# Attention: probabilities times values in plain f32, even and odd key blocks in two 64-column tiles, instead of high and low parts

## The chip, the cores and the metric

The kernel runs on one core of a Trainium2 chip. The metric is the device time of one execution in microseconds (us); lower is better. The engines are named as in the profile: PE multiplies matrices, DVE and ACT work element by element and can read PSUM, POOL works element by element on SBUF, SP starts the transfers. Every engine takes its instructions in its own order.

## The reference

Two layers over 2048 positions of width 1024, batch 1, all in float32. Layer 0 runs a recurrent branch and an attention branch side by side; layer 1 is a state-space layer. The change lies in the attention of layer 0: 8 heads of 64 value columns, causal, keys of 96 (64 and 32 rotated).

```python
def _mla_attention(q_nope, q_rope, k_nope, k_rope, v):
    scale = (MLA_NOPE + MLA_ROPE) ** -0.5
    for blk in range(seqlen // Q_BLOCK):
        ...
        s = (jnp.einsum('bqhd,bkhd->bhqk', q_nope[:, q0:kend], k_nope[:, :kend])
             + jnp.einsum('bqhr,bkr->bhqk', q_rope[:, q0:kend], k_rope[:, :kend]))
        s = jnp.where(mask, s.astype(jnp.float32) * scale, -jnp.inf)
        p = jax.nn.softmax(s, axis=-1).astype(v.dtype)
        outs.append(jnp.einsum('bhqk,bkhd->bqhd', p, v[:, :kend]))
```

The result of the attention is multiplied by a gate and then by an output matrix (`ab_w_out`), 1024 by 1024.

## The kernel before, in words

Most products run in a reduced f32 type (`F32R`) on operands that were split into a high and a low part: the high part is a cast to that type, the low part what the cast left out. `lo` (line 128) makes the low part by a subtraction, `mm3` (line 131) adds the three products high times high, high times low and low times high.

**Work before the attention.** `qkv_begin` and `phase_qkv` make the keys, the values and the queries from two compressed inputs. `vunit` (602) makes one block of 128 positions of all heads' values: three matmuls, then for even and for odd heads a cast on ACT to the high part and a subtraction on DVE for the low part, written to `W`, the large weight buffer of ten slots. There the values of one head and one key block are 128 columns: 64 high and 64 low, in an order that depends on the head's parity. Eight of the 16 value blocks are made in `qkv_begin`, eight in `phase_qkv` beside the first eight query units, whose results leave through four staging tiles `qf` and the queue of SP.

**The attention.** `phase_attn` goes through 32 groups (`GROUPS`): head pair `pr`, chunk `c` of 512 queries, head `e` of the pair. Chunk c sees 4c+4 key blocks of 128, of which the last four are cut by the diagonal. For each group it
- makes the scores of 128 queries against up to 512 keys (`bank`, three matmuls at 741 to 743 and a mask matmul at 745), takes their maxima on DVE (746) and the exponentials on ACT (762) into `prob`;
- transposes 128 by 128 blocks of `prob` on PE (`trans`, 786), up to four for one key block, since the product with the values needs the keys on the partitions;
- casts the transposed block on ACT (792) to a high part and subtracts on DVE (793, by way of line 129) for the low part, into six buffers, four in slots 8 and 9 of `W` and two in `ptx`;
- multiplies (`pv`, 815): the 128 columns of values, high and low together, stay in the array; the high part and then the low part of the probabilities pass through. The accumulator `acc` then has, in one half of its partitions, the values' high part times both parts, and in the other the values' low part times both;
- adds the two halves (821 on ACT, 827 on DVE), multiplies by the gate and by one over the row sum on POOL (824, 831), and stores (834).

**What sets the order.** The program is recorded in the order in which Python calls it. Scores of group n are interleaved with transposes of the group before (loop at 847): after each score bank so many transposes are taken that the ready ones are used up by the end of the group. A `tick` after each step lets deferred work come due: the cast `TL` units after its transpose, the subtraction one later, the exponentials `EL` later. A product follows its transpose `LAG` key blocks later. SP loads the keys of the next head pair (687), the queries two groups ahead (701), and the row sums' and the gate's tiles (811, 812) in between; POOL splits the queries (705 and 129).

**At its end** POOL splits six of the eight slots of output weights (`load_at` at 863) during the last nine groups, into the slots of `W` whose values are used up; the last two are split on ACT and DVE (`last_w`, 866), one of them before the last products are issued. `out0_mm` (916) then reads slot `kb` for block `kb`.

## Time and profile before

| | |
|---|---|
| time, median of 3 runs | 2680.13 us (2680.01 to 2687.45) |
| time of the profiled execution | 2678.24 us |
| its span | 2676.4 us |
| mean granted TensorE clock in it | 0.994 |
| attention in it, first score matmul to last product | 461 to 957 us |
| busy in the whole span: PE, DVE, ACT, POOL | 2610.1, 1749.6, 1531.1, 944.2 us |

The profile comes from one execution. A group of instructions has a line of the program, an engine, an operation, output and input by name, shape, count, and its busy time and mean. A matmul's duration in it holds the time until its result has left the array, so that matmuls which follow each other overlap; how often they follow shows in their start times. An f32 matmul and its loading of weights (PEld) are told apart; "x32" is the number of such records. An entry like `<-DVE W L129` names what ended a wait. In rows of time, the first number is the start in us from the span's start, the second how long the row lasts, to its last record's end.

### The profile page before, as it was taken

The page shows a single profiled execution, that of the slowest core. Times are in us where ns is not written, and L with a number is a line of the kernel's source. Part 1 is how long each engine was busy: PE and PEld are TensorE (multiplying, and loading weights), DVE is VectorE, ACT ScalarE, POOL GpSimd, SP SyncE. Part 2 cuts the span into 40 slices and gives each one's busy share as a digit, 9 for nine tenths or more (in the row PEclk, how much of TensorE's full clock was granted, in tenths as well). Part 3 has the DMA queues.
Part 4 walks back from the last instruction along what each step waited for, and adds up shares of the span by engine and source line. Part 5 has one row for each costly group of instructions (what it writes and reads, how often), then busy time and mean ns, then how long its engine had stood idle before and what let it go on. Part 6 is the DMA issues. An engine that isn't in the chain of part 4 may idle for free.

```text
span 2676.4 us, 40050 instructions
## 1 busy us (share of the span) xinstructions
PE 2610.1 (98%) x14504; PEld 2153.2 (80%) x14504; DVE 1749.6 (65%) x3245; ACT 1531.1 (57%) x3178; POOL 944.2 (35%) x880
## 2 busy tenths in 40 slices
PE   8999999999999999999999999999999999899998
PEld 6888987878787878788888888888888888778886
DVE  7767236878787867875667666666677567745532
ACT  5665335877777732234677766766677667642100
POOL 4446211132324544550334223432343222434421
PEclk9999999999999999999999999999999999999999
DMA  4223328241424456682334333433343333455421
GB/s 140 59 87 118 113 90 284 44 72 43 72 53 85 74 174 196 214 266 95 112 132 159 112 112 108 164 114 112 128 157 123 107 105 118 154 184 210 173 95 40
DMA packets 173111, 334.23 MB, mean 125 GB/s; under 512 B 31985, under 2 KB 90225, under 8 KB 169457
## 3 DMA queue, kind: packets, MB, share of 16 engines
q1 hardware_dynamic: 172912, 331.66, 39.8%
q8 instruction: 115, 1.88, 0.3%
q14 instruction: 84, 0.68, 0.1%
HBM read 245.82 MB, written 85.79 MB: 124 GB/s over the span
## 4 chain that ended last, share of the span: by engine, by line
PE 73%; DVE 10%; ACT 6%; DMA 5%; issue 3%; POOL 1%; SPq 0%; ACTq 0%; POOLq 0%; DVEq 0%
PE ps L1159 9%; PE ps L1161 9%; PE ps L1160 9%; PE ps L137 5%; PE ps L139 4%; PE ps L138 4%; PE ps L786 4%; PE ps L815 4%; PE ps L1409 3%; PE ps L1408 3%; PE ps L1407 3%; PE ps L1262 2%; PE ps L921 2%; PE ps L923 2%; PE ps L922 2%
## 5 line engine op out<-in xcount | busy, mean ns | idle before, releaser
L1159 PE MATMUL ps<-ring,W 128*128 128x512 f32 x768 | 304.6, 397 | 0.0
L1161 PE MATMUL ps<-ring,W 128*128 128x512 f32 x768 | 300.1, 391 | 0.0
L1160 PE MATMUL ps<-ring,W 128*128 128x512 f32 x768 | 299.2, 390 | 0.0
L746 DVE TENSOR_REDUCE mx<-ps 128x1 f32<-128x512 f32 (+3 forms) x320 | 193.5, 608 | 73.9 <-PE ps L743 48.7
L1281 POOL TENSOR_TENSOR y<-y,xs 128x512 f32<-128x512 f32 x60 | 78.8, 1313 | 427.6 <-DVE y L1280 427.6
L762 ACT ACTIVATE pr<-ps,mx 128x512 f32<-128x512 f32 (+3 forms) x320 | 198.5, 629 | 15.8 <-DVE mx L750 11.0
L1159 PE MATMUL ps<-W,ring 128*128 128x512 f32 x512 | 201.3, 393 | 0.0
L1161 PE MATMUL ps<-W,ring 128*128 128x512 f32 x512 | 200.3, 391 | 0.0
L1160 PE MATMUL ps<-W,ring 128*128 128x512 f32 x512 | 199.9, 390 | 0.0
L786 PE MATMUL ps<-cst,pr 128*128 128x128 f32 x1088 | 176.6, 277 | 8.1 <-ACT pr L762 5.9
L1212 ACT ACTIVATE e<-e,tab 128x128 f32<-128x128 f32 x512 | 156.4, 390 | 41.8 <-DMA e<-d_cs 41.8
L1161 PEld LDWEIGHTS ps<-ring,W 128*128 128x128 f32 x768 | 144.1, 188 | 31.2
L1159 PEld LDWEIGHTS ps<-ring,W 128*128 128x128 f32 x768 | 144.3, 188 | 29.7 <-ACT yo L1313 0.9
L1160 PEld LDWEIGHTS ps<-ring,W 128*128 128x128 f32 x768 | 144.4, 188 | 28.9
L129 DVE TENSOR_TENSOR W<-ps,W 128x512 fp32r<-128x512 f32 (+3 forms) x261 | 145.0, 561 | 30.8 <-ACT W L613 18.8
L786 PEld LDWEIGHTS ps<-cst,pr 128*128 128x128 f32 x1088 | 130.6, 142 | 42.0 <-ACT pr L762 11.0
L1127 ACT ACT_TABLE_LOAD x58 | 74.4, 1283 | 149.0 <-DVE xT L1125 79.2
L1392 ACT CAST ring<-ring 128x1024 fp32r<-128x1024 f32 x50 | 50.3, 1045 | 188.7 <-PE ps L1408 99.3
L129 POOL TENSOR_TENSOR ring<-ring 128x1024 fp32r<-128x1024 f32 (+1 forms) x41 | 84.5, 2062 | 189.0 <-ACT ring L1392 160.1
L792 ACT CAST W<-ps 128x512 fp32r<-128x512 f32 (+2 forms) x213 | 110.8, 526 | 67.0 <-PE ps L786 63.0
L129 POOL TENSOR_TENSOR W<-st,W 128x512 fp32r<-128x512 f32 (+2 forms) x70 | 111.4, 1598 | 105.0 <-ACT W L112 90.2
L1125 DVE SCALAR_TENSOR_TENSOR xT<-ps,vec,xT 128x509 f32<-128x509 f32 (+2 forms) x192 | 143.2, 746 | 5.0
(347 smaller groups left out, 7509.7 us busy)
## 6 DMA issues: line engine op xcount, KB each, us to landing
ring<-d_x1T SPq DMA_DIRECT2D x128, 512.0 KB, 7.4
e<-d_cs SPq DMA_DIRECT2D x64, 512.0 KB, 4.4
ring<-d_y SPq DMA_DIRECT2D x25, 1024.0 KB, 4.8
st<-in_w_dram SPq DMA_DIRECT2D x40, 512.0 KB, 5.7
d_x1T<-xt SPq DMA_DIRECT2D x32, 512.0 KB, 4.0
d_y<-yo SPq DMA_DIRECT2D x64, 256.0 KB, 4.9
st<-in_wo_dram SPq DMA_DIRECT2D x24, 512.0 KB, 3.8
xs<-in_xT_dram SPq DMA_DIRECT2D x23, 512.0 KB, 3.9
```

The lines of the kernel that those rows point to most:

```text
L129: eng.tensor_tensor(out=out, in0=src, in1=hi.bitcast(F32), op=ALU.subtract)
L137: self.nc.tensor.matmul(ps, ah, bh, start=(i == 0), stop=False)
L138: self.nc.tensor.matmul(ps, ah, bl, start=False, stop=False)
L746: v.tensor_reduce(out=m[:, kc:kc + 1], in_=ps[:, 0:nw], axis=AX.X, op=ALU.max, negate=True)
L762: nc.scalar.activation(out=prob[n][:, o:o + nw], in_=ps[:, 0:nw], func=AF.Exp, bias=nm, accum_out=acc)
L786: nc.tensor.transpose(ps[:, i * 128:i * 128 + 128], prob[n][:, o:o + 128], self.ident)
L792: self.later(TL, lambda: nc.scalar.copy(hl[:, 0, w], ps[:, w]))
L1125: v.scalar_tensor_tensor(out=dst, in0=src, scalar=w(k), in1=dst, op0=ALU.mult, op1=ALU.add)
L1159: nc.tensor.matmul(ps, ah, bh, start=(k == 0), stop=False)
L1160: nc.tensor.matmul(ps, ah, bl, start=False, stop=False)
L1161: nc.tensor.matmul(ps, al, bh, start=False, stop=(k == KB - 1))
L1212: nc.scalar.activation(out=e[:, hd], in_=e[:, hd], func=AF.Relu, scale=-1.0, bias=cs[:, hd:hd + 1])
```

## The change

The values stay whole f32 numbers: a value block is copied from PSUM by one instruction on ACT to a staging tile and brought to its place in `W` by a transfer on SP's queue (512 pieces of 512 bytes). They take four slots of `W` instead of eight. A transposed block of probabilities is copied once, as f32, by ACT for even and by DVE for odd key blocks, into a buffer `pts` of six places; the cast and the subtraction are gone. Products come for two key blocks at a time: the even block's matmul has the head's 64 value columns in one half of the array's columns and writes one half of the accumulator's partitions, the odd block's matmul has its 64 in the other half and writes the other. The sum of both halves is taken as before, except where chunk 0's odd blocks reach only columns from 128 on. `LAG` is 4 instead of 5, and a product is issued only behind an odd block. The slots of the output weights are renumbered (`WO`), so that seven are split on POOL from the tenth-last group on, and only one is left for the end.

```diff
 GROUPS = [(pr, c, e) for pr in range(4) for c in ((3, 0, 1, 2) if pr == 3 else (3, 2, 1, 0)) for e in range(2)]
 
 
-EL, TL, LAG, SLACK = 3, 1, 5, 4
+WO = (4, 5, 6, 7, 0, 1, 2, 3)
+
+
+EL, TL, LAG, SLACK = 3, 1, 4, 4
+
+NPT = 6
 
 GL, GT, RT = 3, 3, 5
 
...
 
+    def values(self):
+
+        return self.W[:, 0:4, :].bitcast(F32).rearrange("p a (k n) -> p a k n", n=128)
+
     def qkv_begin(self):
 
         nc, A, v = self.nc, self.A, self.nc.vector
-        vv = self.W[:, 0:8, :].rearrange("p (a b) (k n) -> p a b k n", b=2, n=128)
+        vv = self.values()
         cT = self.cT
         self.cnt = 0
+        self.vtile = lambda: self.a2.tile([P, 512], F32, tag="cn", name="cn", bufs=4)
 
         def vunit(tt):
             c, t = divmod(tt, 4)
             ps = self.psum()
             s = cT[c][:, :, 2, t * 128:t * 128 + 128]
             self.mm3(ps, [((s[:, 0], s[:, 1]), (self.wkv[:, 0, 512:1024], self.wkv[:, 1, 512:1024]))])
-            p4 = ps.rearrange("p (a b n) -> p a b n", b=2, n=64)
 
             def post():
-                for b in range(2):
-                    hi = vv[:, :, b, tt, 64 * b:64 * b + 64]
-                    lo = vv[:, :, b, tt, 64 - 64 * b:128 - 64 * b]
-                    nc.scalar.copy(hi, p4[:, :, b])
-                    self.lo(v, lo, p4[:, :, b], hi)
+                f = self.vtile()
+                nc.scalar.copy(f, ps)
+                nc.sync.dma_start(out=vv[:, :, tt], in_=f.rearrange("p (a n) -> p a n", n=128))
             self.later(1, post)
 
         def kunit(pr, c):
...
     def phase_qkv(self):
         nc, p = self.nc, self.a3
         cT, D = self.cT, self.D
+        self.vtile = lambda: p.tile([P, 512], F32, tag="qf", name="qf", bufs=4)
         T = {}
 
         def factors(c):
...
 
     def phase_attn(self):
         nc, A, p, v = self.nc, self.A, self.at, self.nc.vector
-        vv = self.W[:, 0:8, :].rearrange("p h (k n) -> p h k n", n=128)
+        vv = self.values()
+        pts = p.tile([P, NPT, 512], F32, name="pts")
         ring, D = self.ring, self.D
         N = len(GROUPS)
 
         im = self.im
-        ptx = p.tile([P, 2, 1024], F32R, name="ptx")
 
         g, li, y = (p.tile([P, 512], F32, name=k) for k in ("g", "li", "y"))
         half = lambda e: slice(64 * e, 64 * e + 64)
...
                 o = 512 * c * i + 64 * i * (i + 1) + kb * 128
                 nc.tensor.transpose(ps[:, i * 128:i * 128 + 128], prob[n][:, o:o + 128], self.ident)
             self.cnt += 1
-            k = self.cnt % 6
-            hl = self.W[:, 8 + k // 2, k % 2 * 1024:k % 2 * 1024 + 1024] if k < 4 else ptx[:, k - 4]
-            hl = hl.rearrange("p (s n) -> p s n", s=2)
+            pt = pts[:, self.cnt % NPT]
             w = slice(128 * i0, 512)
-            self.later(TL, lambda: nc.scalar.copy(hl[:, 0, w], ps[:, w]))
-            self.later(TL + 1, lambda: self.lo(v, hl[:, 1, w], ps[:, w], hl[:, 0, w]))
-            flow.append((n, kb, hl, w))
+            copy = v.tensor_copy if kb % 2 else nc.scalar.copy
+            self.later(TL, lambda: copy(pt[:, w], ps[:, w]))
+            flow.append((n, kb, pt, w))
             if kb == 4 * c + 3:
                 prob[n] = None
-            if len(flow) > LAG:
+            if len(flow) > LAG and kb % 2:
                 pv()
             self.tick()
 
         def pv():
 
-            n, kb, hl, w = flow.pop(0)
+            (n, kb, *_), (_, kb1, *_) = two = [flow.pop(0) for _ in range(2)]
             pr, c, e = GROUPS[n]
             nkb = 4 * c + 4
             if kb == 0:
                 accs[n] = self.psum()
-            if kb == max(3, nkb - 8):
+            if kb == max(2, nkb - 8):
 
                 end[e]()
                 nc.sync.dma_start(out=li[half(e)], in_=D["li"][n].partition_broadcast(64))
                 nc.sync.dma_start(out=g[half(e)], in_=D["sg"][pr, half(e), c * 512:c * 512 + 512])
             acc = accs[n]
-            for s in range(2):
-                nc.tensor.matmul(acc[:, w], vv[:, 2 * pr + e, kb], hl[:, s, w],
-                                 start=(kb == 0 and s == 0), stop=(kb == nkb - 1 and s == 1))
-            if kb == nkb - 1:
-                r, o = half(e), half(1 - e)
+            r, o = half(e), half(1 - e)
+            for (_, b, pt, w), rows in zip(two, (r, o)):
+                nc.tensor.matmul(acc[rows, w], vv[:, pr, b, half(e)], pt[:, w], start=b < 2, stop=b >= nkb - 2)
+            if kb1 == nkb - 1:
+
+                w = slice(0 if c else 128, 512)
 
                 def copy():
-                    nc.scalar.copy(y[r], acc[o])
+                    nc.scalar.copy(y[r, w], acc[o, w])
+
+                def add():
+                    v.tensor_tensor(out=y[r, w], in0=y[r, w], in1=acc[r, w], op=ALU.add)
+                    if c == 0:
+                        v.tensor_copy(y[r, 0:128], acc[r, 0:128])
+                    accs.pop(n)
 
                 def gate():
                     nc.gpsimd.tensor_tensor(out=g[r], in0=g[r], in1=li[r], op=ALU.mult)
-
-                def add():
-                    v.tensor_tensor(out=y[r], in0=y[r], in1=acc[r], op=ALU.add)
-                    accs.pop(n)
 
                 def fin():
                     nc.gpsimd.tensor_tensor(out=y[r], in0=y[r], in1=g[r], op=ALU.mult)
...
                     trans()
             if pr < 3:
                 self.load_k(pr + 1, c, e)
-            k = n - (N - 9)
-            if 0 <= k < 6:
-                self.load_at(0, k, A["wo0"][k], 7, (nc.gpsimd, nc.gpsimd))
-        k, old, ws = 0, True, []
-
-        def last_w(i):
-            nc.scalar.copy(self.W[:, 6 + i, 0:1024], ws[i])
-            self.lo(v, self.W[:, 6 + i, 1024:2048], ws[i], self.W[:, 6 + i, 0:1024])
+            k = n - (N - 10)
+            if 0 <= k < 7:
+                self.load_at(0, WO[k], A["wo0"][k], 7, (nc.gpsimd, nc.gpsimd))
+        k, ws = 0, []
 
         def read_w():
-            for i in range(2):
-                ws.append(self.stp.tile([P, 1024], F32, tag="st", name="st"))
-                nc.sync.dma_start(out=ws[i], in_=A["wo0"][6 + i])
+            ws.append(self.stp.tile([P, 1024], F32, tag="st", name="st"))
+            nc.sync.dma_start(out=ws[0], in_=A["wo0"][7])
         todo = [(0, read_w), (1, lambda: [self.out0_load(tt) for tt in range(4)]),
                 (6, lambda: self.out0_split(0)), (8, lambda: self.out0_split(1))]
         while ready or flow or any(d[1].__qualname__.endswith("expo") for d in self.defer):
             while todo and todo[0][0] <= k:
                 todo.pop(0)[1]()
-            if old and k > 3 and not any(x[0] < N - 1 for x in ready + flow):
-                old = False
-                self.later(2, lambda: last_w(0))
             k += 1
             if ready:
                 trans()
...
                 self.tick()
         for _, fn in todo:
             fn()
-        if old:
-            last_w(0)
-        last_w(1)
+        hi, lo = self.W[:, WO[7], 0:1024], self.W[:, WO[7], 1024:2048]
+        nc.scalar.copy(hi, ws[0])
+        self.lo(v, lo, ws[0], hi)
 
         ps = self.out0_ps = [self.psum(), self.psum()]
         for hf in range(2):
...
         r, n0 = 2 * (tt % 3), half * 512
         for kb in range(k0, k1):
             ah, al = (self.ring[:, r + s, kb * 128:kb * 128 + 128] for s in range(2))
-            bh, bl = self.W[:, kb, n0:n0 + 512], self.W[:, kb, 1024 + n0:1536 + n0]
+            bh, bl = self.W[:, WO[kb], n0:n0 + 512], self.W[:, WO[kb], 1024 + n0:1536 + n0]
             self.nc.tensor.matmul(ps, ah, bh, start=(kb == 0), stop=False)
             self.nc.tensor.matmul(ps, ah, bl, start=False, stop=False)
             self.nc.tensor.matmul(ps, al, bh, start=False, stop=(kb == KB - 1))
```

PE's order in the attention, before the change, where a group with several chunks of keys is under way (786 transposes, 815 products, 741 to 743 scores):

```order
L786 MATMUL ps<-cst,pr 128x128 x4
L815 MATMUL ps<-W 128x512 x2
L741 MATMUL ps<-ring 128x512
L742 MATMUL ps<-ring 128x512
L743 MATMUL ps<-ring 128x512
L786 MATMUL ps<-cst,pr 128x128 x4
L815 MATMUL ps<-W 128x512 x2
L741 MATMUL ps<-ring 128x512
```

And after it, in such a place (794 transposes, 822 products, 749 to 751 scores):

```order
L794 MATMUL ps<-cst,pr 128x128 x4
L822 MATMUL ps<-pts,W 64x512 x2
L749 MATMUL ps<-ring 128x512
L750 MATMUL ps<-ring 128x512
L751 MATMUL ps<-ring 128x512
L794 MATMUL ps<-cst,pr 128x128 x4
L749 MATMUL ps<-ring 128x512
L750 MATMUL ps<-ring 128x512
L751 MATMUL ps<-ring 128x512
L794 MATMUL ps<-cst,pr 128x128 x4
L822 MATMUL ps<-pts,W 64x512 x2
```

Two products stood behind every transposed key block; now two stand behind every second one, of different key blocks. The 160 pairs come in 158 places, of which 128 have transposes ahead and scores behind, 29 transposes on both sides, and the last one three pairs in a row.

SP's order in the stage that makes the queries, after the change (702 and 695 load keys, 673 stores queries, 621 brings values to their place):

```order
L702 DMA ring<-d_kr 64x1024
L695 DMA ring<-d_k 64x1024
L673 DMA d_q<-qf 128x512
L621 DMA W<-qf 128x4x128
L702 DMA ring<-d_kr 64x1024
L695 DMA ring<-d_k 64x1024
L673 DMA d_q<-qf 128x512
L621 DMA W<-qf 128x4x128
```

The transfer of values is new in each of the first eight steps; before, the three others stood there without it.

## The prediction

> **What bounds the kernel now.** I read first the page's span and chain of waits, then the busy time per engine over the attention (461 to 957 us, first to last use of the changed lines), then PE's order in time inside it.
>
> ```profile
> span 2676.4 us, 40050 instructions
> PE 73%; DVE 10%; ACT 6%; DMA 5%; issue 3%; POOL 1%; SPq 0%; ACTq 0%; POOLq 0%; DVEq 0%
> ```
>
> ```profile
> core 0: us, PE busy (x) PEld busy (x) DVE busy (x) ACT busy (x) POOL busy (x), PEclk, DMA share, GB/s
> 500.00:550.00 50.00, 49.87 (x311) 42.74 (x310) 42.25 (x95) 39.09 (x101) 10.24 (x9) 1.00 0.25 43
> 550.00:600.00 50.00, 45.63 (x266) 38.27 (x264) 38.05 (x91) 34.74 (x99) 18.38 (x17) 0.97 0.51 81
> ...
> 461.00:957.30 496.30, 473.22 (x2821) 398.70 (x2819) 403.76 (x900) 376.28 (x998) 162.30 (x142) 0.99 0.36 69
> ```
>
> The chain is PE's for 73% of the span. In the attention PE is busy 473.2 of 496.3 us, so no more than 23.1 us there is idle; where the key blocks are many (500 to 550) it is busy 49.9 of 50, and the idle time sits where they are few (550 to 600). DVE (403.8) and ACT (376.3) have room. So the attention is PE's, and what matters is what PE does with the products of probabilities and values.
>
> **The products themselves.** The busy time of a matmul holds its latency, so I price by start to start. PE's order in time, columns start, time, engine, line:
>
> ```profile
> 522.29 0.60 PE L786 MATMUL ps<-cst,pr 128*128 128x128 f32 x4
> 522.65 0.71 PE L815 MATMUL ps<-W 128*128 128x512 f32 x2
> 523.20 0.39 PE L741 MATMUL ps<-ring 128*128 128x512 f32 x1
> 523.43 0.40 PE L742 MATMUL ps<-ring 128*128 128x512 f32 x1
> ...
> 523.89 0.60 PE L786 MATMUL ps<-cst,pr 128*128 128x128 f32 x4
> 524.25 0.59 PE L815 MATMUL ps<-ptx,W 128*128 128x384 f32 x2
> 524.68 0.34 PE L741 MATMUL ps<-ring 128*128 128x384 f32 x1
> ...
> 525.27 0.60 PE L786 MATMUL ps<-cst,pr 128*128 128x128 f32 x4
> 525.63 0.48 PE L815 MATMUL ps<-ptx,W 128*128 128x256 f32 x2
> 525.95 0.39 PE L741 MATMUL ps<-ring 128*128 128x512 f32 x1
> ...
> 526.65 0.60 PE L786 MATMUL ps<-cst,pr 128*128 128x128 f32 x4
> 527.01 0.42 PE L815 MATMUL ps<-W 128*128 128x128 f32 x2
> 527.26 0.44 PE L741 MATMUL ps<-ring 128*128 128x512 f32 x1
> ```
>
> From the first of four transposes to the next score matmul is 0.91 us. Four transposes take 0.44 (0.60 less the last one's own 0.27 is three steps of 0.11), so one key block's two products cost 0.47 at 512 columns; by the same subtraction 0.35 at 384, 0.24 at 256, 0.17 at 128. A group of chunk c has 4c+4 key blocks, the last four of them narrowing; over 32 groups that is 320 blocks: 96 pairs (512, 512), 32 pairs (512, 384) and 32 pairs (256, 128), at 0.94, 0.82 and 0.41.
>
> After the change a pair is two f32 matmuls of 64 columns in two tiles. The kernel has this form already, at L1262 with 64 moving columns, and a plain f32 matmul over the whole array at L1223:
>
> ```profile
> 1490.88 0.27 PE L1222 MATMUL ps<-cst,B 128*128 128x128 f32 x1
> 1490.99 0.39 PE L1223 MATMUL ps<-C,B 128*128 128x128 f32 x2
> 1491.13 0.47 PE L1159 MATMUL ps<-W,ring 128*128 128x512 f32 x1
> ...
> 1501.91 0.39 PE L1161 MATMUL ps<-ring,W 128*128 128x512 f32 x1
> 1502.23 1.15 PE L1262 MATMUL ps<-xf,e 128*64 128x64 f32 x32
> 1503.31 0.50 PE L137 MATMUL ps<-hl,ch 128*128 128x512 f32 x1
> 1503.65 0.39 PE L138 MATMUL ps<-hl,ch 128*128 128x512 f32 x1
> ```
>
> One f32 matmul is two records (L1223: one call, x2; L1262: 16 calls, x32). At 128 columns the second record starts 0.11 after the first (0.39 less one record's own 0.27 to 0.28). At L1262, 32 records start within 1.15 - 0.23 = 0.92 us: were they one after another, that would be 0.030 each, less than the 0.055 that half of 0.11 makes for 64 columns; so they run two at a time, one in each tile, 15 steps of about 0.06. A record of 512 columns is not in the trace. Four times the 128-column record is 0.44, eight times the 64-column step 0.49, the line through both 0.40; I take 0.43, near the row closest in kind per column, so 0.86 for a pair with 512 and 0.43 (twice 0.215) for (256, 128). Streams: 96 x (0.86 - 0.94) + 32 x (0.86 - 0.82) + 32 x (0.43 - 0.41) = **-5.8 us** (bounds: about -13 at 0.40 and +11 at 0.49). The sum of products costs PE almost what it cost.
>
> **The switch between tilings.** This is the term that decides. In the L1262 rows, L1161 to L138 is 1.74 us. In it are two matmuls of 0.23 (their usual step, as from L741 at 523.20 to L742 at 523.43) and 16 steps, 0.98. What is left, **0.30 us**, is paid once per visit: 0.09 before the first tile matmul (0.32 after L1161 instead of 0.23), the rest behind the last one, where L137 starts late and its follower comes 0.34 instead of 0.23 later, since the next weights were not loaded ahead. A visit of 64-column matmuls in one tile alone shows less:
>
> ```profile
> 990.68 0.39 PE L923 MATMUL ps<-W,ring 128*128 128x512 f32 x1
> 990.90 1.12 PE L1012 MATMUL ps<-xt,wdt 128*64 128x128 f32 x16
> 991.86 0.45 PE L921 MATMUL ps<-W,ring 128*128 128x512 f32 x1
> 992.15 0.40 PE L922 MATMUL ps<-W,ring 128*128 128x512 f32 x1
> ```
>
> 1.47 us, less 0.46 and 16 steps of 0.06, leaves 0.05. The Trainium skill says in TensorEngine Tiling (Array Packing), Key Properties, that changing the tiling mode, and not just the tile, drains TensorE. The trace agrees at L1262, and does not at L1012, whose columns are as few; a rule that held for every 64-column matmul would give 0.30 at both.
>
> The changed form is L1262's: f32, both tiles. PE's order shows one pair between transposes and scores nearly everywhere: 160 pairs in 158 visits. 158 x 0.30 = **+47.4 us** (bounds: 158 x 0.05 = +8, and +55 if the first weights, which L1262 also pays, come on top at 0.05). I take 0.30: same type, same two tiles.
>
> **What DVE and ACT get back.** Each transposed block had a cast on ACT (L792) and a subtraction on DVE (L129); now one copy, on ACT for even blocks and on DVE for odd ones.
>
> ```profile
> 461.00:957.30 496.30, 192.10 (x323) 57.26 (x44) 0.99 0.36 69
> ...
> 461.00:957.30 496.30, 165.53 (x320) 0.99 0.36 69
> ```
>
> The first row is L129 (DVE, POOL), the second L792 (ACT). DVE loses 192 us and, if a copy costs it what a subtraction did, gains back half, 96; ACT loses half of 165.5. That leaves DVE about 308 and ACT about 293 us busy of 496. That is not on PE's chain in the dense stretches. It can only shorten the 23.1 us of PE's idle time. The largest pieces of it, of three like this one, are:
>
> ```profile
> 573.76 0.59 PE L815 MATMUL ps<-W 128*128 128x384 f32 x2
> 576.93 0.33 PE L741 MATMUL ps<-ring 128*128 128x128 f32 x1 [2.58 <-POOL ring L705]
> ```
>
> There the queries' load is issued late, because in SP's queue it stood behind the store of the row sums, and that behind DVE's subtractions, as SP's waits from 540 to 585 us have it:
>
> ```profile
> SPq L775 <- DVE W L129: 2.7, 1, 2.7
> ```
>
> With DVE lighter, and PE slower by some 2 us on the way there, I take **-8 us** of stalls (bounds 0 and -23). The added wait is that of the pair for the copy on DVE; behind it on PE stand the next scores. It is covered: four transposed blocks, over 2 us of PE's work, lie between a copy and its product (LAG 4), against about 0.7 for the copy.
>
> **Values and weights.** Sixteen value blocks get one ACT copy and one 256 KB transfer in place of two casts and two subtractions; eight of these transfers fall where the DMA engines are full.
>
> ```profile
> 410.00:440.00 30.00, 29.62 (x124) 22.52 (x124) 15.51 (x30) 16.08 (x36) 0.00 (x0) 1.00 1.03 328
> ```
>
> DMA share 1.03 at 328 GB/s, PE still busy 29.6 of 30. Eight transfers of 256 KB at that rate are 6.4 us; the queries' four staging buffers now serve both, so part of it may reach PE. I take **+2** (bounds -1 and +6.4). At the end of the attention one of the two late splits of output weights no longer stands in front of the last copies:
>
> ```profile
> 954.30 0.50 PE L815 MATMUL ps<-W 128*128 128x512 f32 x1 [1.37 <-DVE W L129]
> ```
>
> That wait goes: **-1.4**. The seventh split on POOL (162 of 496 us busy) costs nothing.
>
> **Sum.** -5.8 + 47.4 - 8 + 2 - 1.4 = +34.2 on the profiled execution's 2678.2 (2676.4 of span) is 2712.4; that execution lies 1.9 under the median 2680.1, so **2714 us**, 1.3% slower. Own range of this case, by the bounds not all at one end: 2692 to 2745.
>
> **Rivals.**
>
> *The switch is cheap*, as at L1012. For it: no drain there, with as narrow weights. Against: another type and a single tile. Then -5.8 + 8 - 8 + 2 - 1.4 = -5, about 2675, no measurable change.
>
> *Relief decides, and it is faster.* If the switch is cheap and the lighter DVE and ACT also take 20 of the 23.1 us of idle time: -5.8 + 8 - 20 - 1.4 = -19, 2661. Its place is the groups with one or two chunks of keys, 550 to 600 and its like; it decides from the point where stalls won exceed 158 times the visit. At 0.30 they can't: 23 is less than 47.
>
> *The two tiles don't overlap.* L1262's two tiles read the same moving block xf; the change gives each tile another one. If that forces them one after another, each pair costs the second product too: 96 x 0.86 + 32 x 0.65 + 32 x 0.22 = +110, about 2824. For it, only that the trace shows no two streams of different data; against it, that each record of L1262 fetches its moving operand for itself. The Trainium skill gives in TensorE: Matmul & The Clock Gate, Measured speedup vs the span model, 2.38 times for three column tiles at 512 columns; an estimate from that page makes a pair 0.86 x 3 / 2.38 = 1.08 and the time near 2745. No run here shows it.
>
> **Chances.** Forecast 0.66; cheap switch 0.14; faster by relief 0.08; no overlap 0.12. The first two lie in 2668 to 2745 nearly whole, 0.79 together with the edges of the others; that is my range. A measurement of this kernel tells a change from none at about 0.3%, 8 us. Faster by more than that: 0.08 and a third of the cheap switch, 0.13. Within it: most of the cheap switch and the low edge of the forecast, 0.10. Slower: 0.77.
>
> **What would show it.** In the changed profile: two records of each tile starting together, about 0.43 apart, at the new product line (else the no-overlap rival); transposes to tile matmul and tile matmul to score matmul each about 0.1 later than their streams end, with the follower 0.34 instead of 0.23 behind (else the cheap switch); DVE near 308 and ACT near 293 us in the attention; the attention longer by some 33 us and everything after 960 us unchanged. The prediction is wrong if the attention is not longer, or by more than 65 us.

## The result and the profile after

The changed kernel takes 2709.73 us (median of 4 runs, 2704.89 to 2713.47) against 2681.48 us for the kernel before beside it (4 runs): a ratio of 1.010 with a 95% interval of 1.0074 to 1.0127, so 1% slower. The prediction was 2714 us. The profiled execution took 2704.89 us. The span and the chain of waits on the page of after:

```profile
span 2702.8 us, 39360 instructions
...
PE 80%; DVE 7%; DMA 5%; ACT 5%; issue 2%; POOL 1%; SPq 1%; ACTq 0%; POOLq 0%; DVEq 0%
```

Busy time by engine, the same three stretches as before (the last is the whole attention, which now begins at 470.1 us and ends at 983.3):

```profile
core 0: us, PE busy (x) PEld busy (x) DVE busy (x) ACT busy (x) POOL busy (x), PEclk, DMA share, GB/s
500.00:550.00 50.00, 50.00 (x279) 31.13 (x279) 29.64 (x67) 28.49 (x76) 12.01 (x11) 1.00 0.19 42
550.00:600.00 50.00, 49.76 (x292) 31.34 (x289) 29.06 (x75) 27.59 (x75) 13.69 (x13) 1.00 0.44 72
470.10:983.30 513.20, 502.78 (x2818) 323.82 (x2816) 321.71 (x747) 310.04 (x836) 164.18 (x145) 1.00 0.34 66
```

DVE and ACT fell by 82 and 66 us, as they should. PE is now almost without a gap even between 550 and 600 us (49.76 of 50), and the attention is 17.6 us longer all the same. Around one pair of products (columns start, time, engine, line):

```profile
521.79 0.60 PE L794 MATMUL ps<-cst,pr 128*128 128x128 f32 x4
522.32 1.08 PE L822 MATMUL ps<-pts,W 128*64 128x512 f32 x4
523.33 0.50 PE L749 MATMUL ps<-ring 128*128 128x512 f32 x1
523.67 0.40 PE L750 MATMUL ps<-ring 128*128 128x512 f32 x1
523.91 0.39 PE L751 MATMUL ps<-ring 128*128 128x512 f32 x1
```

Transposes to products: 0.53, of which 0.44 is the four transposes' own, so 0.09 late. The products stand for 1.01 until the score matmul; two records of 0.43 are 0.86, so 0.15 more. The follower comes 0.34 later instead of 0.23, 0.11 more. Together **0.35 us per visit**. The instruction records behind the row with x4 start in pairs, one in each tile, 6 to 7 ns apart (where the two blocks differ in width, the two records that start together have the two widths), and the second pair follows the first by 0.48: two tiles with different moving blocks do run side by side.

To see the rest I split PE's time in the attention in two. Every step from one matmul's start to the next is set against the usual length of such a step (the tenth percentile of steps with the same neighbours). The usual lengths add up to "work", what goes beyond them to "waits". Unlike PE's idle time, this also counts waits that are hidden in a matmul's latency and matmuls that run on a slower clock. The split depends a little on what counts as the same neighbours: where their widths must agree too, the groups are smaller and the waits come out at 46.5 and 18.6 us instead of 52.9 and 21.1. Differences of a few us between waits say nothing here.

| us | before | after | difference |
|---|---|---|---|
| attention begins | 461.6 | 470.1 | +8.5 |
| attention, work of PE | 442.7 | 492.1 | +49.4 |
| attention, waits of PE | 52.9 | 21.1 | -31.8 |
| behind the attention | 1719.2 | 1719.5 | +0.3 |
| span | 2676.4 | 2702.8 | +26.4 |

The work is 158 visits x 0.35 = +55.3, less 5.9 for the streams. The 8.5 us ahead of the attention arise where the value blocks are moved (the row of before for this stretch, 29.62 of 30 us busy, is in the prediction):

```profile
410.00:420.00 10.00, 8.76 (x36) 6.46 (x36) 1.21 (x2) 5.61 (x10) 0.00 (x0) 1.00 1.02 371
420.00:430.00 10.00, 6.18 (x16) 4.48 (x17) 1.38 (x2) 2.36 (x4) 0.00 (x0) 0.66 1.07 274
430.00:440.00 10.00, 7.05 (x29) 4.81 (x28) 2.07 (x3) 2.95 (x5) 0.00 (x0) 1.00 1.06 274
```

PE in the order of time there:

```profile
418.43 0.40 PE L144 MATMUL ps<-wkv,cT 128*128 128x512 f32 x1
423.82 0.79 PE L142 MATMUL ps<-cT,W 128*128 128x512 f32 x1 [4.99 <-ACT qf L672]
424.41 0.63 PE L143 MATMUL ps<-cT,W 128*128 128x512 f32 x1
```

The DMA engines are full (share 1.02 to 1.07). DVE waits 11.2 us for the store that empties a staging tile `qf`, ACT waits for DVE (7.4 us) and PE for ACT. Behind the wait the matmuls follow each other by 0.43 instead of 0.23: the granted clock is 0.66 in this slice. One trace each does not fix the 8.5 us to better than a few: in the traces of this case whose kernels have the same stages ahead of it, the attention begins at 461.6 to 465.3 us in the form of before (four traces) and at 469.3 to 476.6 in the form of after (eight).

Medians of the kernel before on the chips used below lie between 2681 and 2691 us. So I compare times by their ratio to the runs of before beside them, and, between traces, work and waits rather than tenths of a length.

### The profile page after: what moved, and what is told of

Its sections match the earlier page's. It is cut to its first block, busy times and chain, and to the rows that moved or that the text cites. A ratio compares the mean times of both kernels' runs of the same rounds, so it can differ in the third digit from the quotient of the medians.

```text
span 2702.8 us, 39360 instructions
## 1 busy us (share of the span) xinstructions
PE 2644.7 (98%) x14504; PEld 2082.8 (77%) x14504; DVE 1652.3 (61%) x3060; ACT 1464.1 (54%) x3001; POOL 944.4 (35%) x883
## 3 DMA queue, kind: packets, MB, share of 16 engines
q8 instruction: 114, 1.87, 0.3%
## 4 chain that ended last, share of the span: by engine, by line
PE 80%; DVE 7%; DMA 5%; ACT 5%; issue 2%; POOL 1%; SPq 1%; ACTq 0%; POOLq 0%; DVEq 0%
PE ps L1160 10%; PE ps L1162 10%; PE ps L1161 10%; PE ps L142 5%; PE ps L144 5%; PE ps L143 5%; PE ps L822 4%; PE ps L794 4%; PE ps L1409 4%; PE ps L1408 4%; PE ps L1410 4%; PE ps L749 2%; PE ps L1263 2%; PE ps L922 2%; PE ps L923 2%; PE ps L924 2%
## 5 line engine op out<-in xcount | busy, mean ns | idle before, releaser
L1160 PE MATMUL ps<-ring,W 128*128 128x512 f32 x768 | 304.7, 397 | 0.0
L1160 PE MATMUL ps<-W,ring 128*128 128x512 f32 x512 | 201.3, 393 | 0.0
L794 PE MATMUL ps<-cst,pr 128*128 128x128 f32 x1088 | 167.6, 275 | 4.7 <-ACT pr L770 4.7
L1160 PEld LDWEIGHTS ps<-ring,W 128*128 128x128 f32 x768 | 144.3, 188 | 29.6 <-ACT yo L1314 0.9
L799 ACT COPY pts<-ps 128x512 f32<-128x512 f32 (+1 forms) x160 | 86.9, 543 | 135.5 <-PE ps L794 134.3
L822 PE MATMUL ps<-pts,W 128*64 128x512 f32 (+3 forms) x640 | 158.1, 553 | 0.0
```

The source lines that it names most:

```text
L794: nc.tensor.transpose(ps[:, i * 128:i * 128 + 128], prob[n][:, o:o + 128], self.ident)
L822: nc.tensor.matmul(acc[rows, w], vv[:, pr, b, half(e)], pt[:, w], start=b < 2, stop=b >= nkb - 2)
L1160: nc.tensor.matmul(ps, ah, bh, start=(k == 0), stop=False)
```

## The experiments

### What a visit costs

**Half as many visits.** Four key blocks per visit instead of two, with room for eight transposed blocks; the gate's and the row sums' tiles move into `W`.

```diff
-NPT = 6
+NPT = 8
...
-        g, li, y = (p.tile([P, 512], F32, name=k) for k in ("g", "li", "y"))
+        y = p.tile([P, 512], F32, name="y")
+        g, li = (self.W[:, 8, 512 * k:512 * k + 512].bitcast(F32) for k in range(2))
...
-            if len(flow) > LAG and kb % 2:
+            if len(flow) > LAG and kb % 4 == 3:
+                pv()
                 pv()
...
-                    nc.gpsimd.tensor_tensor(out=g[r], in0=g[r], in1=li[r], op=ALU.mult)
+                    nc.gpsimd.tensor_tensor(out=y[r], in0=y[r], in1=li[r], op=ALU.mult)
```

> The changed kernel with products issued for four key blocks at a time (two pairs in a row) instead of two; buffers for transposed blocks 8 instead of 6, and to make room the gate and row-sum tiles lie in an unused slot of the weight buffer (the result is multiplied by the one and then by the other). The visits of PE to the 64-column tiles fall from 158 to 79; the products stay the same. Theory, the price is per visit (0.35 us each in the trace of the changed kernel: 0.09 before, 0.06 for the first weights, 0.09 behind, 0.11 for the follower): 79 x 0.35 = 28 us less, about 2677 against 2705. Rival, the price lies in the 64-column f32 products themselves: no change, 2705. Rival, longer visits hold up the scores and so DVE and ACT: part of the 28 us comes back as stalls, 2685 to 2700.

Measured: ratio 1.0079 (1.0053 to 1.0104). There are 79 visits, and PE's work fell from 492.1 to 463.8: 28.3 us, or 0.358 for each visit gone, as the expectation's theory has it. But the waits rose from 21.1 to 59.6 and the attention took 523.4, as its last rival has it and further. The gating had been changed too, so I repeated it with the gating left as it was.

**The same, with only the row sums' tile moved.**

```diff
-NPT = 6
+NPT = 7
...
-        g, li, y = (p.tile([P, 512], F32, name=k) for k in ("g", "li", "y"))
+        g, y = (p.tile([P, 512], F32, name=k) for k in ("g", "y"))
+        li = self.W[:, 8, 0:512].bitcast(F32)
...
-            if len(flow) > LAG and kb % 2:
+            if len(flow) > LAG and kb % 4 == 3:
+                pv()
                 pv()
```

> As visit2, four key blocks a visit, but with seven buffers for transposed blocks and only the row-sum tile moved to the unused weight slot, so that POOL multiplies the gate by one over the row sum ahead of the result, as in the changed kernel. In visit2 PE's work from start to start fell by 28.3 us in the attention as the theory had it, but its waits rose from 21 to 60 us, 26 us of them scores that waited for POOL's split of the queries. Theory, those waits came from the moved multiplication on POOL: they go here, the waits are near 21 us, the attention is near 485 us (513 less 28) and the time about 1% under the changed kernel's, level with the kernel before. Rival, waits grow because PE is faster and nothing hides them: PE's work 464 us, waits 40 us or more, attention above 500 us.

Measured: ratio 1.0086 (1.0068 to 1.0104). Work 464.2, waits 49.3, attention 513.5: to 0.3 us as long as after. This is the rival: with the gating left in place the waits are only 10 us lower. One visit of four blocks in PE's order:

```profile
521.45 0.60 PE L795 MATMUL ps<-cst,pr 128*128 128x128 f32 x4
521.98 1.94 PE L824 MATMUL ps<-pts,W 128*64 128x512 f32 x8
523.85 0.33 PE L750 MATMUL ps<-ring 128*128 128x128 f32 x1
```

It is again 0.53 to the products, and 1.87 for twice 0.86: the visit's cost is paid once, whatever its length. So the 0.35 us are a price per visit, and 28 us of them can be taken away; but in this kernel they come back as waits.

**Both products in one tile.** The odd block's product goes to the even one's columns, so the two run one behind the other; an even head uses one tile throughout, an odd head the other. The accumulator's halves are then not added (not in the lines below).

```diff
-            for (_, b, pt, w), rows in zip(two, (r, o)):
-                nc.tensor.matmul(acc[rows, w], vv[:, pr, b, half(e)], pt[:, w], start=b < 2, stop=b >= nkb - 2)
+            for _, b, pt, w in two:
+                nc.tensor.matmul(acc[r, w], vv[:, pr, b, half(e)], pt[:, w], start=b == 0, stop=b == nkb - 1)
```

> The changed kernel with both products of a pair in the same 64-column tile, one after the other, so that a group uses one tile alone, the first half of the columns for even heads and the second for odd ones; the accumulator's halves needn't be added. What it tells apart: the gaps of 0.09 us before and behind a visit. Theory A, they come from 64-column f32 products as such: they stay, for both halves. Theory B, they come from changing between two tile positions: they are gone for even heads at least, as at the reduced-f32 product of 64 columns in layer 0's last stage (0.05 in all). In both, the second product of each pair is no longer covered: 110 us more, attention about 620 us, time about 2815; if the tiles had not overlapped in the changed kernel, no more than now.

Measured, in a single run: 2815.01 us beside a median of 2687.6 before. Work 601.9, 109.8 more than after, which is what the prediction's rival without overlap put it at.

```profile
493.77 0.60 PE L794 MATMUL ps<-cst,pr 128*128 128x128 f32 x4
494.30 1.93 PE L822 MATMUL ps<-pts,W 128*64 128x512 f32 x4
496.16 0.50 PE L749 MATMUL ps<-ring 128*128 128x512 f32 x1
496.50 0.40 PE L750 MATMUL ps<-ring 128*128 128x512 f32 x1
```

0.53 ahead, 1.86 for the products, 0.34 for the follower. Ahead of the products every one of the 158 visits shows a step of 0.20 from the last transpose instead of 0.11, whether its tile is the first or the second half of the columns. So the price does not come from using two tiles, nor from changing between them.

The type alone could be a rival, since the products are f32 and the scores reduced. The kernel before settles it at L1223, f32 over the whole array with a reduced matmul behind it (the transpose ahead of it, at 1490.88, is in the prediction):

```profile
1490.99 0.39 PE L1223 MATMUL ps<-C,B 128*128 128x128 f32 x2
1491.13 0.47 PE L1159 MATMUL ps<-W,ring 128*128 128x512 f32 x1
1491.44 0.39 PE L1160 MATMUL ps<-W,ring 128*128 128x512 f32 x1
```

From 1490.88 to 1491.44 is 0.56, and the usual steps make 0.56 too: 0.11 for the transpose, twice 0.11 for the f32 records, 0.23 for L1159. L1160 comes late there as well (0.31 instead of 0.23), but L1159 had started as much too early, so nothing is paid. The 0.35 of a visit therefore holds only as a sum; its piece "follower 0.11 late" is in part the change of type, which starts the matmul ahead of it early. What is paid for is going from 128-column to 64-column matmuls and back, in f32. Why L1012, 64 columns in the reduced type, shows only 0.05 stays open.

### What the waits were

**Before without the subtractions.** The low part of the probabilities is left out: DVE makes none, and the second product uses the high part again. PE does the same number of matmuls.

```diff
-            self.later(TL + 1, lambda: self.lo(v, hl[:, 1, w], ps[:, w], hl[:, 0, w]))
...
-                nc.tensor.matmul(acc[:, w], vv[:, 2 * pr + e, kb], hl[:, s, w],
+                nc.tensor.matmul(acc[:, w], vv[:, 2 * pr + e, kb], hl[:, 0, w],
```

> The kernel before without its 320 subtractions on DVE in the attention: the second product of each key block reads the high part again, so that PE's and ACT's work stays and the probabilities' low part is left out. Theory, the 32 us of stalls that the change won back in the attention were mostly waits behind these subtractions, not behind the queue of SP at the change of head pairs: 18 to 28 us less than before, 2650 to 2660. Rival, DVE had room enough (404 of 496 us busy) and the stalls went because a slower PE hides them: within 5 us of 2678. Rival, half of it is ACT's casts: about 12 us less.

**After with a subtraction.** Each transposed block gets a subtraction on DVE again, whose result nobody reads.

```diff
             self.later(TL, lambda: copy(pt[:, w], ps[:, w]))
+            self.later(TL + 1, lambda: self.lo(v, self.W[:, 8, w], ps[:, w], pt[:, w]))
```

> The changed kernel with one more subtraction on DVE for each transposed block, as the kernel before had it; its result is not read. DVE's copies of odd blocks stay, so DVE has about 90 us more than before the change had. Theory, waits behind DVE decide the stalls: the attention gets 20 to 35 us longer, 2725 to 2740. Rival, a slower PE hides them: less than 8 us more, below 2713.

Measured: ratios 0.9937 (0.9922 to 0.9951) and 1.0167 (1.0148 to 1.0186). The attention of the first, then of the second:

```profile
463.70:946.00 482.30, 464.67 (x2817) 397.58 (x2816) 245.85 (x580) 373.36 (x998) 161.05 (x142) 0.99 0.39 71
```

```profile
476.60:1014.60 538.00, 512.97 (x2817) 327.21 (x2816) 477.92 (x1066) 309.37 (x836) 164.08 (x145) 0.99 0.35 64
```

Without the subtractions DVE is busy 245.9 instead of 403.5 us, and the waits fall from 52.9 to 39.2; the attention is 13.3 us shorter, below the 18 to 28 that were expected. With one added to after, DVE is busy 477.9 and the waits rise from 21.1 to 44.8; the work stays (493.1). So DVE's load is worth 13.7 us of waits measured from before and 23.7 measured from after (a load that is 18% above before's there). The change won 31.8; some 8 of them or more are something else. ACT's lighter load and PE's slower pace, which both changed too, were not tried apart.

### The values' way

**Values written by ACT straight into place**, without a staging tile and a transfer. They are rounded to the reduced type by it, so their low parts are left out.

```diff
-                f = self.vtile()
-                nc.scalar.copy(f, ps)
-                nc.sync.dma_start(out=vv[:, :, tt], in_=f.rearrange("p (a n) -> p a n", n=128))
+                nc.scalar.copy(self.W[:, 0:4, tt * 128:tt * 128 + 128], ps.rearrange("p (a n) -> p a n", n=128))
```

> The changed kernel without the sixteen transfers of values: ACT writes each value block straight to its place, rounded to the reduced f32 type, since that buffer takes no other from ACT. The values' low parts are left out by this; the count and size of PE's work stays. Theory, the 8.5 us by which the attention starts later than before come from these transfers in a stage whose DMA engines are full: the attention starts at about 462 instead of 470 us, and the time falls by 8 to 9 us to about 2696. Rival, they come from the staging tiles or from ACT's longer copies, or from the order of the queue of SP alone: less than 3 us.

Measured: ratio 1.006 (1.0038 to 1.0081). The attention begins at 456.3, 13.8 us earlier than after (8 to 9 were expected) and 5.3 earlier than before.

```profile
410.00:420.00 10.00, 10.00 (x44) 8.07 (x44) 2.50 (x4) 4.35 (x8) 0.00 (x0) 1.00 1.03 312
420.00:430.00 10.00, 10.00 (x45) 8.05 (x44) 2.20 (x4) 3.58 (x7) 0.00 (x0) 1.00 1.04 294
430.00:440.00 10.00, 8.60 (x37) 6.31 (x36) 4.13 (x6) 3.87 (x7) 0.00 (x0) 1.00 0.79 244
```

PE works almost without a gap. So the sixteen transfers, with the staging tiles that they hold, cost 13.8 us, and the lighter ACT and DVE give back some 5 of them; both by one trace each, and so to within a few us.

**The transfers spread out.** The shorter visits above, and the second half of the value blocks beside every fourth query unit instead of each of the first eight.

```diff
-            if n < 16 - 4 * VB:
-                self.vunit(4 * VB + n)
+            if n % 4 == 3:
+                self.vunit(4 * VB + n // 4)
                 self.tick()
```

> visit2b, with the eight value blocks of the query stage spread over its 32 steps (one in every four) instead of the first eight, so that their transfers do not all fall where the DMA engines are full and the staging tiles wait. Without any value transfers the attention started 13.8 us earlier. Theory, the transfers hold PE because they come in the full stretch: the attention starts 4 to 10 us earlier than the changed kernel's 470, and the time is 4 to 10 us under visit2b's, below the kernel before. Rival, the stage is limited by the sum of its transfers: no change against visit2b.

Measured: ratio 1.0078 (1.006 to 1.0096), against 1.0086 without the spreading; the attention begins at 471.5, no earlier. From 410 to 440 us PE is busy 21.27 of 30 and the DMA share is 1.04: as the rival has it, the stage goes by the sum of its transfers, and not by where they stand. That their sum is what holds it is argued from the full DMA engines; no run lessens the sum alone.

### Where the shorter visits' gain went

In the kernel with 79 visits and only one tile moved, the waits sit at the ends of the head pairs, where groups have few keys: 10.4 us of 49.3 fall between 575 and 600, 10.2 between 700 and 750, some 11 between 825 and 875. There:

```profile
584.45 0.38 PE L795 MATMUL ps<-cst,pr 128*128 128x128 f32 x2
590.33 0.47 PE L750 MATMUL ps<-ring 128*128 128x128 f32 x1 [5.50 <-POOL ring L713]
```

PE waits for POOL's split of the next queries, and POOL for the queries. I took SP's order for the cause: at 580 us SP stood 7.2 us at the load of the row sums, which waits for their store, with a queries' load behind it.

**The row sums one block earlier**, in the kernel before:

```diff
-            if kb == max(3, nkb - 8):
+            if kb == max(2, nkb - 8):
```

> The kernel before, with one number changed: for chunk 0 the row sums and the gate are fetched, and the work on the group two before is finished, one key block earlier (at block 2 instead of 3), where the changed kernel does it too. Theory, the three waits of 1.5 to 2.6 us at the change of head pairs and what follows them, some 10 us of the 32 us of waits that the change won back, come from that place: the scores' wait for POOL's split of the queries goes, the attention is 8 to 12 us shorter than before's 496. Rival, they come from ACT's or DVE's load or from PE's pace: less than 3 us.

Measured, in a single run: 2691.95 us beside a median of 2687.6; waits 61.4. The expected 8 to 12 us do not show.

**The queries' path taken out of the queues.** ACT and DVE split the queries instead of POOL; POOL's queue takes the loads of row sums and gate and the store of the output from SP's. It was done to three kernels: the one with 79 visits, after, and before.

```diff
-        nc.gpsimd.tensor_scalar(out=t[:, 0:512], in0=st, scalar1=1.0, scalar2=0.0, op0=ALU.mult, op1=ALU.add)
-        self.lo(nc.gpsimd, t[:, 512:1024], st, t[:, 0:512])
+        nc.scalar.copy(t[:, 0:512], st)
+        self.lo(nc.vector, t[:, 512:1024], st, t[:, 0:512])
...
-                nc.sync.dma_start(out=li[half(e)], in_=D["li"][n].partition_broadcast(64))
-                nc.sync.dma_start(out=g[half(e)], in_=D["sg"][pr, half(e), c * 512:c * 512 + 512])
+                nc.gpsimd.dma_start(out=li[half(e)], in_=D["li"][n].partition_broadcast(64))
+                nc.gpsimd.dma_start(out=g[half(e)], in_=D["sg"][pr, half(e), c * 512:c * 512 + 512])
...
-                nc.sync.dma_start(out=D["y0"][4 * c:4 * c + 4, r, 4 + pr, :].rearrange("t p n -> p t n"),
+                nc.gpsimd.dma_start(out=D["y0"][4 * c:4 * c + 4, r, 4 + pr, :].rearrange("t p n -> p t n"),
```

> As the kernel with four key blocks to a visit and the row sums' tile moved (ratio 1.0086, attention 513.5 us, work 464.2, waits 49.3), with the queries' path taken out of two queues: their split into high and low parts is done by ACT (32 copies) and DVE (32 subtractions) instead of POOL, and the loads of 1/row sum and of the gate and the store of the gated output are issued on POOL's queue instead of SP's, so that the queries' load stands behind none of them. The computation is unchanged. Theory (a chain of fixed pace over SP's queue and POOL at the ends of the groups, row sums' store, their load, gate, output's store, and behind them the queries of the next group, is what the faster PE ran into): the PE work stays at 464, the waits fall from 49 to 20 to 28, attention takes 485 to 492 us, and the ratio is 0.997 to 1.000. Rival (PE waits for the chain of each block on DVE and ACT, whose hand-overs the shorter visits no longer hide): the waits stay at 45 or more, ratio 1.007 to 1.011.

> The same three edits on the changed kernel (two blocks to a visit, ratio 1.010, attention 513.2 us, work 492.1, waits 21.1). Theory of the chain: few waits are left there that it could cause, so they fall by 4 to 10 us only, attention takes 503 to 509 us and the ratio is 1.006 to 1.009: the slower PE had hidden most of the chain. Rival: nothing moves, ratio 1.010.

> The same three edits on the kernel before (attention 495.6 us, work 442.7, waits 52.9, of which leaving out DVE's subtractions took 13.7). DVE gets some 19 us more work in attention, ACT some 14. Theory of the chain: of the 39 us of waits that were left without the subtractions about half are the chain's, so the waits fall by 12 to 22 us, attention takes 474 to 484 us and the ratio is 0.992 to 0.996. Rival (the waits that are left are those of DVE and ACT, which only get more work): ratio 1.000 to 1.003.

Measured, in this order: 1.0164 (1.0142 to 1.0186), 1.018 (1.0158 to 1.0202), 1.0122 (1.0107 to 1.0137). All three are slower than what they were made from, and slower than theory and rival both had it; the waits rose to 71.6, 42.0 and 87.3. Two of the first one's groups of waits:

```profile
ACT ring L713 <- DMA st<-d_q: 29.4, 10, 4.4
...
ACT y L830 <- DMA d_y<-y: 25.1, 4, 10.7
```

The queries still were not there, and the engine that now stood waiting for them was ACT, with exponentials and copies behind it. Since ACT and DVE also got some 16 and 20 us of work, these runs don't test SP's order cleanly. That took one more.

**Only the order.** For the groups of chunks 0 and 1 of the kernel with 79 visits, the loads of row sums and gate go behind the next queries' load, and the gating behind the next splits of queries. No engine gets other work.

```diff
                 end[e]()
-                nc.sync.dma_start(out=li[half(e)], in_=D["li"][n].partition_broadcast(64))
-                nc.sync.dma_start(out=g[half(e)], in_=D["sg"][pr, half(e), c * 512:c * 512 + 512])
+
+                def fetch():
+                    nc.sync.dma_start(out=li[half(e)], in_=D["li"][n].partition_broadcast(64))
+                    nc.sync.dma_start(out=g[half(e)], in_=D["sg"][pr, half(e), c * 512:c * 512 + 512])
+                if c > 1:
+                    fetch()
+                else:
+                    self.later(6, fetch)
...
-                for at, k in ((4, 2), (6, 1), (10, 0)) if c else ((8, 2), (10, 1), (14, 0)):
+                for at, k in ((4, 2), (6, 1), (10, 0)) if c > 1 else ((16, 2), (18, 1), (22, 0)):
```

> As the kernel with four key blocks to a visit and the row sums' tile moved (ratio 1.0086, attention 513.5 us, work 464.2, waits 49.3), with only an order changed, and no engine given other work: for the groups of query chunks 0 and 1 the loads of 1/row sum and gate are issued six units of the schedule later, behind the next queries' load on SP's queue, and the gating 16 units behind the end of the products, so that POOL splits the queries of the next two groups before it gates. The computation is unchanged. At 580 us of that kernel SP stood 7.6 us at the row sums' load with the queries' load behind it, and PE waited 5.5 us for their split. Theory (SP's order makes the queries late, and that is most of the 16.9 us of waits between transposes and scores): the queries' load is issued some 7 us earlier there, those waits fall to 6 us or less, attention takes 499 to 506 us and the ratio is 1.003 to 1.006. Rival (at the short groups something else is as late, the keys' landing or the output tile that is still being stored, and only takes the queries' place): attention takes 511 us or more and the ratio is 1.008 or more.

Measured: ratio 1.0177 (1.0155 to 1.0199). Waits 73.3, attention 537.3; the waits between transposes and scores 18.2 instead of 16.9. SP and POOL in the order of time, two fences of the kernel with 79 visits, then two of this one:

```profile
577.73 0.54 SPq L709 DMA_DIRECT2D st<-d_q  x1
...
587.56 0.45 SPq L819 DMA_DIRECT2D W<-d_li  x1
...
588.74 0.54 SPq L709 DMA_DIRECT2D st<-d_q  x1
```

```profile
589.66 0.62 POOL L713 TENSOR_SCALAR ring<-st 128x512 fp32r<-128x512 f32 x1 [8.41 <-DMA st<-d_q]
```

```profile
577.02 0.54 SPq L709 DMA_DIRECT2D st<-d_q  x1
...
580.75 0.45 SPq L709 DMA_DIRECT2D st<-d_q  x1
586.83 0.45 SPq L821 DMA_DIRECT2D W<-d_li  x1
```

```profile
589.65 0.62 POOL L713 TENSOR_SCALAR ring<-st 128x512 fp32r<-128x512 f32 x1 [11.91 <-DMA st<-d_q]
```

The second queries' load is issued 8.0 us earlier, at 580.75 instead of 588.74, as wanted. But the split that PE waits for takes the queries issued at 577.73 (577.02 here), and it starts at 589.65 as it did at 589.66. That load had not stood behind the loads that were moved. It had been issued, and its transfer took 12 us. **For this wait my theory of SP's order falls.** Another transfer did stand in front of it: SP waited 5.0 us for the output's store at 576.42, and that for POOL's gating. But in the first of the three kernels above, where that store is not on SP's queue, the load was issued at 575.37 and its split started at 587.78, only 2.4 and 1.9 us earlier. From the load's issue to its split it is 11.9, 11.9 and 11.3 us at the ends of the first three head pairs with 79 visits, and 11.4, 11.0 and 11.7 after, where PE waits less than 1 us for it. The trace's packets bear it out: between 582 and 588 us in the kernel with 79 visits, packets of 4096 bytes, half of which elsewhere in the attention take no more than 0.16 us, took up to 5.7 us, and the ten that took more than 1.5 us ended together between 588.3 and 588.7. Before and after have such clusters too, near the ends of the head pairs and, before, in other places. What holds the transfers there I have not found; a store of row sums, 2 KB in pieces of 4 bytes, runs into this stretch, but no run takes it away.

The run also shows why it got slower still: the gated output is stored later, and ACT waits for its tile:

```profile
ACT y L836 <- DMA d_y<-y: 26.1, 3, 12.1
```

This is the expectation's rival, that something as late takes the queries' place, and the time is well above what even the rival needs.

**What is shown, then:** a faster PE reaches the short groups sooner and waits there for transfers that take 11 to 12 us either way. Halving the visits won 28 us of work and lost 28 of waits; the slower PE of the changed kernel hides them. **What is not shown:** why the transfers are slow there, and so how to keep the 28 us. No version with the whole computation beat the kernel before.

## Why the prediction was right, and by which steps

The time was 4 us off and the change slower, as forecast. But three terms were mis-sized, and that the total came so close is in part luck: the errors of two of them cancelled most of the third's. On the span, where after's profiled execution lies 4.8 us under its median, the miss is 7.8 us.

- **Streams, -5.8.** Measured -5.9, as what is left of the work's +49.4 less 158 x 0.35. The steps bear it out: a visit's products take 1.00 us up to the next matmul at 512 columns and 0.58 at 256, and less the 0.15 that the visit adds there this is 0.86 and 0.43, as taken. (The lower bound's own sum at 0.40 is -14, not -13.)
- **Switch, 158 x 0.30 = +47.4.** Measured 158 x 0.35 = +55.3, the upper bound (+55). The 0.30 taken from L1262 was too small by the first weights, 0.05 to 0.06, which stood in its bound; halving the visits confirmed 0.35. The Trainium skill says in TensorEngine Tiling (Array Packing), Key Properties, that a change of the tiling mode drains TensorE while a change of tile does not: by that rule the price is the same with one tile or with two, and the one-tile run agrees, 0.20 instead of 0.11 ahead of every visit in either tile. L1012 changes the width as well and pays 0.05, so the rule alone gives no price.
- **Stalls, -8 and -1.4.** Measured -31.8, outside the bound of -23. The step that failed is "It can only shorten the 23.1 us of PE's idle time." PE's idle time is not all its waiting. A matmul's busy time holds its latency, about 0.17 us of which hides a short wait; and 6.1 us of before's waits were matmuls at half the clock, which count as busy. The waits were 52.9. DVE's subtractions account for 13.7 to 23.7 of what was won; the largest remaining piece lies at the ends of the head pairs. There the prediction had the queries' load late because of the store of the row sums, and that because of DVE's subtractions. The trace of before shows it at one place of three: SP stood 2.6 us at that store ahead of the load of 564.95, and at most 0.2 us ahead of those of 689.57 and 813.46. From issue to split all three loads took 10.2 to 11.3 us. And without the subtractions the kernel before kept 39.2 us of waits.
- **Values' transfers, +2, at most +6.4.** Measured +8.5 net, 13.8 for the transfers alone. The bound took eight transfers at the stage's rate and left out what the wait behind a staging tile does to PE: it stands 4.99 us and then runs 5 us at half the clock.
- **Late split, -1.4.** The waits between products, where it stood, fell from 3.3 to 0.4; they are contained in the -31.8.
- **The sum:** -5.9 + 55.3 - 31.8 + 8.5 + 0.3 = +26.4 on the span, against +34.2 forecast. Switch and transfers were 14.4 too small, the stalls' relief 22.4.
- **The signs named beforehand:** second records 0.43 apart plus 0.05 to 0.06, a step of 0.34 to the follower, nothing changed behind the attention: all there. DVE came to 321 and ACT to 310 us, not 308 and 293; the attention is 17.6 us longer, not 33.
- **The rivals.** A cheap switch is refuted by 0.35 per visit. Relief that decides is refuted, though relief was larger than its bound: 31.8 is still less than 55.3. Two tiles that don't overlap are refuted by starts 6 to 7 ns apart; the one-tile run shows what that would have cost, +109.8 us of work. The Trainium skill's 2.38 for three tiles, in TensorE: Matmul & The Clock Gate, Measured speedup vs the span model, made a pair 1.08 by estimate; the trace has 0.86 plus the visit's 0.15 behind it.

## What to carry to other kernels

Price a change of matmul width by the visit, from a place in the trace where the same type changes width and goes back, including the step to the first matmul and the step behind the next one; then count visits, not matmuls. Bound what a relief can win by the waits measured from start to start, not by the idle time of an engine whose records overlap and whose clock can fall. And before you move a load ahead in a queue, check from issue and landing of that very load whether it was late because it stood or because it took long.

## What the runs showed of the hardware

**A wait costs more than itself.** In the attention, half clock comes in stretches of 3.4, 6.8 and 10.2 us behind PE's long waits. The kernel with 79 visits around its wait at 585 us:

```profile
585.00:587.00 2.00, 0.00 (x0) 0.00 (x0) 0.34 (x1) 1.02 (x3) 0.00 (x0) 1.00 0.33 27
...
590.00:591.00 1.00, 0.67 (x2) 0.50 (x2) 0.00 (x0) 0.00 (x0) 0.92 (x2) 0.50 0.60 70
...
592.00:594.00 2.00, 2.00 (x8) 1.17 (x9) 0.38 (x2) 0.00 (x0) 0.00 (x0) 0.50 0.17 30
594.00:596.00 2.00, 2.00 (x8) 0.96 (x5) 0.29 (x1) 0.54 (x1) 0.00 (x0) 0.50 0.31 41
```

The granted clock is 0.50 from 590.0 on, for 6.8 us. Half the time that PE was busy in such stretches of the attention, an estimate of what they cost, is 6.1 us before (three stretches), nothing after, 9.9 with 79 visits, and 15.4 with the changed order. The Trainium skill, in TensorE: Matmul & The Clock Gate, What's actually happening, has half rate after an idle window of about 3.4 us. The stretches agree with that length; but in the kernel before the clock fell at 578.5, behind a wait of 2.58 us (in the prediction) and one of 0.91 with two matmuls between them, so here no wholly idle window of that length stood ahead of it:

```profile
578.27 0.33 PE L743 MATMUL ps<-ring 128*128 128x128 f32 x1 [0.91 <-POOL ring L129]
```

**A load of queries takes 11 us beside the attention**, and 2.9 us in the stage before it, for the same 256 KB, by the median from issue to landing. First before, then after, 480 to 984 us, then after, 400 to 460 us:

```profile
st<-d_q SPq DMA_DIRECT2D x28, 256.0 KB, 11.1
...
d_li<-ls SPq DMA_DIRECT2D x31, 2.0 KB, 12.0
```

```profile
st<-d_q SPq DMA_DIRECT2D x29, 256.0 KB, 10.8
...
d_li<-ls SPq DMA_DIRECT2D x32, 2.0 KB, 9.4
```

```profile
st<-d_q SPq DMA_DIRECT2D x2, 256.0 KB, 2.9
```

The small store of row sums, in 512 pieces of 4 bytes, takes as long as the large load. Whether the one makes the other slow was not tried.
